# A decoder layer's SBUF pools laid out anew: where the moving operands of the matmuls begin

## Chip, cores and metric

The kernel runs on one core of a Trainium2 chip. The metric is the device time of one execution in microseconds; the median of three runs of the kernel before is 1162.74 us (1161.46 to 1162.74).

## What is computed

The reference is one decoder layer on x [512 tokens, 1024], float32:

```python
x = x + 0.5 * swiglu(rmsnorm(x, norm_ffn1), ffn1_gate, ffn1_up, ffn1_down)      # d_ff = 2816
h = rmsnorm(x, norm_mix)
qa, ka, va, qb, kb, vb, g_a, g_b = split(h @ w_in)
y_a = dilated_window_attention(qa, ka, va)     # 12 heads of 64, three groups merged
y_b = moba_attention(qb, kb, vb)               # 8 heads of 64, causal at this length
merged = sigmoid(g_a) * (y_a @ w_up_a) + sigmoid(g_b) * (y_b @ w_up_b)
x = x + merged @ w_out
x = x + 0.5 * swiglu(rmsnorm(x, norm_ffn2), ffn2_gate, ffn2_up, ffn2_down)
return rmsnorm(x, norm_final)
```

## The kernel before

The residual stream lies transposed in SBUF: eight tiles x0 to x7 of 128 partitions by 512 tokens. A projection takes a 128x128 piece of the weights as the stationary operand and a tile of 128x512 (all tokens) as the moving one. Every float32 operand is split into two float32r tiles, hi and lo, and `mac` (L196 to L201) issues three matmuls for each pair: hi*hi (L199), weight hi * moving lo (L200), weight lo * moving hi (L201). So each matmul of a projection has its own weight load, and the moving tiles are xh/xl (the normed stream), ah/al (the activations of the feed-forward halves, 22 pairs, pool `ff0` or `ff2`), yh/yl (the attention's outputs, 6 pairs) and mh/ml (the merged mixers, 8 pairs; both in pool `mrg`).

The stages in order: gate and up of the first half (`ffn(0)`, moving xh/xl), its down projection (moving ah/al), the projections of queries, keys and values and the two attentions with more projections blended in between (`blend`, tables FIRST and BESIDE), gates and merge (`ups`, moving yh/yl), the output projection (moving mh/ml), then the second half in the same way, whose last tile (`last_tile`) is done in two halves of 256 tokens, and the last norm. In `values` (L488 on) the roles are turned: the stream is stationary and 256 columns of the weights (whi/wlo) move; consecutive pieces of 256 columns are 1024 bytes apart.

In the attention the moving operands are ks (keys, from pool `op`) in the score products (L538, L550, L596), the identity in the transposes of the probability rows (L621), and pth/ptl (transposed rows) in the sums of values (L640); the stationary ones are qs, the rows prow and the values v. `bias` (L511) makes a tile of slopes times distances on POOL, read by VectorE when it adds it to the scores; one head of the dilated attention takes two tiles of 256 columns (tags `biasb`, `biasd`), each pair of MoBA heads two tiles of 512 (tag `bias`); every tag has two buffers.

Pools are laid one behind the other in the order in which they are opened, each tag taking its size rounded up to 32 bytes. `cpool`, `xpool`, `wpool` and `tpool` stay open for the whole program; `ff0`, then `op`, `mp` and `mp2`, then `mrg` in place of `mp` and `mp2`, and then `ff2` lie behind `tpool`. The 16-byte columns `rcol` and the 32-byte `nv` are tags of `tpool` (L217, L335), 128 bytes in all, behind its 2048-byte tiles. TensorE's order is written by hand (`manual_schedule`, PE only); the other engines' order is the scheduler's.

Where the tiles begin, in bytes of a partition, in the built program before and in the changed one:

| tiles | first byte before | mod 2048, mod 256 | first byte after | mod 2048, mod 256 |
|---|---|---|---|---|
| x, xh, xl (first: x0) | 18176 | 1792, 0 | 18432 | 0, 0 |
| whi, wlo | 79616 | 1792, 0 | 79872 | 0, 0 |
| tags ssq, fu, fg, rrow of tpool | 96000 | 1792, 0 | 96256 | 0, 0 |
| ah, al | 108416 | 1920, 128 | 108544 | 0, 0 |
| qs, ks (op) | 120704 | 1920, 128 | 120832 | 0, 0 |
| yh, yl (mrg) | 157568 | 1920, 128 | 157696 | 0, 0 |
| mh, ml (mrg) | 182144 | 1920, 128 | 182272 | 0, 0 |
| v | 162720 | 928 or 1952, 160 | 163072 | 256 or 1280, 0 |
| prow | 170912 | 928 or 1952, 160 | 171264 | 256 or 1280, 0 |
| pth, ptl | 212640 | 1696, 160 | 212992 | 0, 0 |
| ident, ones, ones_r | 16640 | 256, 768 or 1280, 0 | 16640 | 256, 768 or 1280, 0 |

Of the kernel before, what the change touches and what calls it, by code (L numbers as in the profile page):

```python
"""One core: a macaron SwiGLU pair around a gated merge of dilated window attention and MoBA.

The residual stream is kept transposed, [d_model on partitions, tokens], so that every projection
takes the weights as the stationary operand and the tokens as the moving one. A float32 operand is
split exactly into two float32r parts (hi + lo, 12 significant bits each); a product is the sum of
hi*hi, hi*lo and lo*hi, added up in float32 in PSUM. Query-key and probability-value products are
small and carry all four parts, hi and lo stacked on the partitions.

The RMSNorm's row factor is applied to the outputs of the projections that follow it, its gain to
their inputs. With MOBA_TOPK >= the number of blocks every past block is selected, so MoBA is causal  # L10
attention here. The three groups of the dilated attention are one softmax over their joint keys.
"""
# [11 lines left out]
F32 = mybir.dt.float32  # L24
# [4 lines left out]
P = 128  # L29
# [8 lines left out]
NT = S // P  # L38
EPS = 1e-6
BIG = 1e30  # L40
# Heads by pairs, as they are projected: those of the dilated attention, then MoBA's.
# [3 lines left out]
def by_class(ap):  # L45
    """[P, tokens] as [P, class t % 4, t // 4]."""
    return ap.rearrange("p (i r) -> p r i", r=NT)
# [10 lines left out]
# The projections of the mixers: those before the attention, and those beside each part of it  # L58
# (scores and weighted sums of each head of the dilated attention, then of each pair of MoBA's).
# [14 lines left out]
def blend(main, side, lead=0):  # L74
    """Run a generator beside others: `lead` steps of the others, then the rest spread over those of `main`.

    Each comes with its number of steps."""
    (main, total), left = main, sum(n for _, n in side) - lead
    steps = (None for g, _ in side for _ in g)
    done = 0  # L80
    for _ in range(lead):
        next(steps, None)
    for at in range(1, total + 1):
        while done * total < left * at:
            next(steps, None)
            done += 1
        next(main, None)
    for _ in main:
        pass
    for _ in steps:  # L90
        pass
# [3 lines left out]
def decoder_layer(ctx: ExitStack, tc: tile.TileContext, xT, gains, gus, gu1, dn1, wqk, wv, wg, wup, wout, gu2, dn2, base, out):  # L95
# [20 lines left out]
    def warm_up(n):  # L116
        """Keep the tensor engine's clock up while it waits."""
        ps = bank("all")
        for _ in range(n):
            nc.tensor.matmul(ps[:, :P], ones, ones, start=True, stop=True)  # L120

# [65 lines left out]
    def weights(*key):  # L187
        """The next tile of the stream, split, with the ones after it on their way."""
        t = state["at"]
        assert stream[t][0] == key, (t, stream[t][0], key)  # L190
        state["at"] += 1
        split(t + 1)
        fetch(t + 3)
        return splits.pop(t)

    def mac(ps, w, x, first, last):  # L196
        """ps += w.T @ x for split operands."""
        (wh, wl), (xh, xl) = w, x
        nc.tensor.matmul(ps, wh, xh, start=first, stop=False)  # L199
        nc.tensor.matmul(ps, wh, xl, start=False, stop=False)  # L200
        nc.tensor.matmul(ps, wl, xh, start=False, stop=last)  # L201
# [8 lines left out]
    def normed(i, k):  # L210
        """Tile k of the stream times the gain, split; and its part of the sum of squares."""
        xh = xpool.tile([P, S], F32R, name=f"xh{i}_{k}", tag=f"xh{k}")
        xl = xpool.tile([P, S], F32R, name=f"xl{i}_{k}", tag=f"xl{k}")
        g = g_sb[:, i * KT + k:i * KT + k + 1]
        nc.scalar.mul(xh, X[k], g)
        nc.vector.scalar_tensor_tensor(xl, X[k], g, f32(xh), ALU.mult, ALU.subtract)
        XN[k] = xh, xl  # L217
# [10 lines left out]
    def newton(y, z, a, out):  # L228
        """out = 1/sqrt(a): a step from the reciprocal of the table's square root."""
# [6 lines left out]
    def factors(i, ps):  # L236
        """1/rms of each token, as rows on all partitions."""
# [14 lines left out]
    def columns(row, dilated):  # L252
        """The same as columns [token of the tile, tile], tiles of 128 tokens or of a class of tokens."""
        col = tpool.tile([P, NT], F32, name="rcol", tag=f"rcol{dilated}", bufs=1)
# [6 lines left out]
    def tokens(x, t, dilated):  # L261
        """Tile t of the tokens of x [P, tokens]."""
        return by_class(x)[:, t] if dilated else x[:, t * P:(t + 1) * P]

# [1 line left out]
    def first_tiles():  # L266
        """Gate and up of the first two tiles, side by side over k as x comes in."""
# [60 lines left out]
    def last_tile(A):  # L328
        """The last tile of the stream in two halves of the tokens, each followed by its part of the output."""
# [6 lines left out]
        v = [tpool.tile([P, 4, 2], F32, name=f"nv{h}", tag=f"nv{h}", bufs=1) for h in range(2)]  # L336
# [92 lines left out]
    with ExitStack() as mix:  # L429
# [5 lines left out]
        consts = mp.tile([P, base.shape[-1]], F32, name="consts", tag="consts")  # L435
        nc.scalar.dma_start(consts, base)
# [8 lines left out]
        def project(t, j, which="acc"):  # L445
            """Queries (j = 0) or keys (j = 1) of a pair of heads, transposed."""
# [6 lines left out]
        def stacked(t, j, ps):  # L453
            v = tpool.tile([P, S], F32, name="qkv", tag="ssq", bufs=1)
            # The scores are kept with the sign turned, as their minimum is then the softmax's bias.
# [8 lines left out]
            # For each head: q as [hi; lo], k as [hi; hi] and [lo; lo].  # L464
# [21 lines left out]
        def values(c):  # L486
            """Values of four heads, tokens on partitions, [hi | lo] per head."""
            # Two tiles of tokens share a bank: its first product clears it for both.  # L488
# [21 lines left out]
        def bias(tag, n, *parts):  # L510
            """Slopes times distances, in [P, n]."""  # L511
            b = mp2.tile([P, n], F32, name="bias", tag=tag)
# [4 lines left out]
        def row_of(row, ps, b, low, den):  # L517
            """exp(score - max) of a row of scores, with its turned maximum and its sum."""
# [3 lines left out]
        def dsa_scores(h, rows):  # L522
            """Rows of the joint softmax of head h of each of the three groups.

            The dilated groups go by the classes t % 4 of the tokens, in which all their keys lie."""
            bb = bias("biasb", 256, (BAND, sl_a[h], 0))
            bd = bias("biasd", 256, (DILATED[:, :P], sl_a[4 + h], 0), (DILATED[:, P:], sl_a[8 + h], P))
            # [low or sum, own or other, by tiles or by classes, tile]
# [5 lines left out]
            for r in range(NT):  # L534
# [5 lines left out]
                # The two parts of the keys side by side: one long product instead of two short ones.  # L540
# [13 lines left out]
            # Each order of the tokens gets the other's minima and sums: a permutation, exact as it adds zeros.  # L554
# [32 lines left out]
        def moba_scores(heads, rows):  # L587
            """Rows of the softmax of each head over all keys up to its own."""
            bs = [bias("bias", 512, (CAUSAL, sl_b[h], 0)) for h in heads]
# [15 lines left out]
        def weighted(steps, ytile, half, classes=False):  # L605
            """The rows' sums of values, transposed, into half a tile of y.

            A step is up to four blocks of the rows to transpose, and the products that they go into:
            (tile of values, columns of y, first column, number of columns). Where the columns of y go by
            classes of tokens, products of 128-token tiles have theirs put into that order."""  # L610
# [47 lines left out]
        def dsa(h):  # L658
            """Scores and weighted sums of a head of the dilated attention, each with its number of steps."""
# [9 lines left out]
            # Tiles 0 and 2 of the keys cover the bank once; the others then add to all that they touch.  # L669
# [9 lines left out]
        def moba(h):  # L679
            """The same of a pair of heads of MoBA."""  # L680
# [31 lines left out]
        def part(what, n, *js):  # L712
            """Projections named in FIRST or BESIDE, with their number of steps."""
# [7 lines left out]
        # The first pair comes before the norm's factor is there.  # L721
# [73 lines left out]
def _tiles(w, heads=None):  # L795
    """[K, N] -> [N/128, 128, K]: for each tile of outputs, its K/128 stationary tiles side by side."""
# [4 lines left out]
def _moving(w, per):  # L801
    """[1024, n] -> [8/per, 128, per * n]."""
# [4 lines left out]
def _base():  # L807
    """Distances to a key, BIG where masked, and permutations of the tokens (see decoder_layer).

    Band of two tiles; classes t % 4 with dilations 4 and 16; all four tiles, ending with the query's."""  # L810
# [64 lines left out]
```

## Time and profile before

| what | value |
|---|---|
| median of the runs | 1162.74 us |
| span of the profiled execution | 1162.7 us |
| PE (matmul) busy | 1150.9 us, 5418 instructions |
| weight loads (PEld) busy | 966.8 us |
| VectorE busy | 597.9 us (51%) |
| ScalarE busy | 413.5 us (36%) |
| HBM traffic | 103.44 MB read, 91 GB/s over the span |

The profile gives no time of its own for this execution beside its span, which is that of the median run to 0.1 us. Matmuls are pipelined: a row's duration reaches into the next row, so the pace of the engine is read from the distance of the starts, and differences of durations between rows are used beside it.

### The profile page before, as it was taken

How to read it: one execution, taken by the hardware profiler on the slowest of the kernel's cores; microseconds unless marked ns; L12 is line 12 of the kernel's file. 1: busy time of each engine (PE TensorE's matmuls, PEld its weight loads, DVE VectorE, ACT ScalarE, POOL GpSimd, SP SyncE). 2: the span in 40 equal slices, each digit the busy share in tenths (PEclk: the TensorE clock that was granted, in tenths of full speed). 3: DMA queues.
4: the chain of work that ended last, by engine and by line, in shares of the span. 5: the costliest groups of instructions: out<-in, count | busy, mean ns of one | idle time of the engine just before them, and what ended most of it. 6: DMA issues, size and time to landing. Idle time of an engine off the chain costs nothing.

```text
span 1162.7 us, 13714 instructions
## 1 busy us (share of the span) xinstructions
PE 1150.9 (99%) x5418; PEld 966.8 (83%) x5418; DVE 597.9 (51%) x975; ACT 413.5 (36%) x641; POOL 19.6 (2%) x35
## 2 busy tenths in 40 slices
PE   8999999999999999999999999999999999999997
PEld 7888888888888899888998888888888888888886
DVE  5745444433333633777677667754744444433223
ACT  5433233222222323544454445433422323322222
POOL 0000000000000100000000000000000000000001
PEclk9999999999999999999999999999999999999999
DMA  5232232233233461446364222332233233233321
GB/s 200 93 107 91 95 105 91 94 97 100 87 99 122 140 173 55 128 127 164 111 162 127 74 64 82 110 99 99 91 96 104 91 96 103 91 100 84 98 82 73
DMA packets 37599, 122.14 MB, mean 105 GB/s; under 512 B 4752, under 2 KB 4768, under 8 KB 37536
## 3 DMA queue, kind: packets, MB, share of 16 engines
q1 hardware_dynamic: 37072, 120.08, 34.3%
q10 hardware_dynamic: 432, 1.18, 0.3%
q8 instruction: 42, 0.69, 0.2%
q14 instruction: 21, 0.17, 0.0%
q0 software_dynamic: 32, 0.02, 0.0%
HBM read 103.44 MB, written 2.10 MB: 91 GB/s over the span
## 4 chain that ended last, share of the span: by engine, by line
PE 98%; DVE 0%; DMA 0%; ACT 0%; issue 0%; DVEq 0%; POOLq 0%
PE ps_all L199 20%; PE ps_all L201 20%; PE ps_all L200 20%; PE ps_acc L199 9%; PE ps_acc L201 9%; PE ps_acc L200 9%; PE ps_all L276 2%; PE ps_out L640 2%; PE ps_att L621 1%; PE ps_att L199 1%; PE ps_att L200 1%; PE ps_att L201 1%; PE ps_att L596 1%; DMA g_sb<-in_gains_dram 0%; PE ps_att L538 0%; PE ps_att L550 0%
## 5 line engine op out<-in xcount | busy, mean ns | idle before, releaser
L182 ACT CAST whi<-raw 128x1024 fp32r<-128x1024 f32 (+2 forms) x201 | 202.8, 1010 | 562.4 <-PE ps_all L200 259.9
L183 DVE TENSOR_TENSOR wlo<-raw,whi 128x1024 fp32r<-128x1024 f32 (+2 forms) x202 | 236.2, 1170 | 174.1 <-ACT whi L182 174.0
L200 PE MATMUL ps_all<-xl,whi 128*128 128x512 f32 x672 | 261.4, 389 | 0.0
L199 PE MATMUL ps_all<-xh,whi 128*128 128x512 f32 x672 | 261.4, 389 | 0.0
L201 PE MATMUL ps_all<-xh,wlo 128*128 128x512 f32 x672 | 261.4, 389 | 0.0
L200 PEld LDWEIGHTS ps_all<-xl,whi 128*128 128x128 f32 x672 | 126.1, 188 | 26.3
L201 PEld LDWEIGHTS ps_all<-xh,wlo 128*128 128x128 f32 x672 | 126.1, 188 | 26.3
L199 PEld LDWEIGHTS ps_all<-xh,whi 128*128 128x128 f32 x672 | 126.1, 188 | 26.0
L199 PE MATMUL ps_all<-ah,whi 128*128 128x512 f32 (+1 forms) x374 | 143.1, 383 | 0.0
L200 PE MATMUL ps_all<-al,whi 128*128 128x512 f32 (+1 forms) x374 | 142.7, 382 | 0.0
L201 PE MATMUL ps_all<-ah,wlo 128*128 128x512 f32 (+1 forms) x374 | 142.7, 382 | 0.0
L199 PE MATMUL ps_acc<-xh,whi 128*128 128x512 f32 x272 | 110.2, 405 | 0.0
L201 PE MATMUL ps_acc<-xh,wlo 128*128 128x512 f32 x272 | 106.9, 393 | 0.0
L200 PE MATMUL ps_acc<-xl,whi 128*128 128x512 f32 x272 | 106.4, 391 | 0.0
L290 DVE TENSOR_TENSOR fu<-ps_all,rrow 128x512 f32<-128x512 f32 x44 | 30.4, 691 | 124.1 <-PE ps_all L201 124.1
L200 PEld LDWEIGHTS ps_all<-al,whi 128*128 128x128 f32 x374 | 70.2, 188 | 15.2
L201 PEld LDWEIGHTS ps_all<-ah,wlo 128*128 128x128 f32 x374 | 70.2, 188 | 15.1
L199 PEld LDWEIGHTS ps_all<-ah,whi 128*128 128x128 f32 x374 | 70.2, 188 | 15.0
L288 DVE TENSOR_TENSOR fg<-ps_all,rrow 128x512 f32<-128x512 f32 x44 | 30.4, 691 | 79.8 <-PE ps_all L201 79.7
L201 PEld LDWEIGHTS ps_acc<-xh,wlo 128*128 128x128 f32 x272 | 51.0, 188 | 11.3
L200 PEld LDWEIGHTS ps_acc<-xl,whi 128*128 128x128 f32 x272 | 51.3, 189 | 7.4
L199 PEld LDWEIGHTS ps_acc<-xh,whi 128*128 128x128 f32 x272 | 51.3, 188 | 7.4
(158 smaller groups left out, 1321.3 us busy)
## 6 DMA issues: line engine op xcount, KB each, us to landing
raw<-in_gu_dram SPq DMA_DIRECT2D x84, 512.0 KB, 3.4
raw<-in_dn_dram SPq DMA_DIRECT2D x32, 512.0 KB, 3.5
raw<-in_wqk_dram SPq DMA_DIRECT2D x20, 512.0 KB, 3.5
ks<-qkhl SPq DMA_DIRECT2D x40, 256.0 KB, 4.9
raw<-in_wg_dram SPq DMA_DIRECT2D x16, 512.0 KB, 3.5
raw<-in_dn_dram SPq DMA_DIRECT2D x16, 384.0 KB, 3.1
raw<-in_wv_dram SPq DMA_DIRECT2D x10, 512.0 KB, 4.0
qs<-qkhl SPq DMA_DIRECT2D x40, 128.0 KB, 2.6
```

Source lines behind the costliest of these rows:

```text
L182: nc.scalar.copy(hi[:, s], raw[:, s])
L183: nc.vector.tensor_tensor(lo[:, s], raw[:, s], f32(hi[:, s]), ALU.subtract)
L199: nc.tensor.matmul(ps, wh, xh, start=first, stop=False)
L200: nc.tensor.matmul(ps, wh, xl, start=False, stop=False)
L201: nc.tensor.matmul(ps, wl, xh, start=False, stop=last)
L276: nc.tensor.matmul(ps[j], w[:, at:at + P], x, start=k == 0 and n == 0, stop=k == KT - 1 and n == 2)
L288: nc.vector.tensor_tensor(g, ps[0], R, ALU.mult)
L290: nc.vector.tensor_tensor(u, ps[1], R, ALU.mult)
L596: nc.tensor.matmul(ps[:, :n], Q[NA + h][:, i * P:(i + 1) * P], K[NA + h][:, part, :n], start=part == 0, stop=part == 1)
L621: nc.tensor.transpose(pt[:, n * P:(n + 1) * P], block, ident)
L640: nc.tensor.matmul(to(po), V[v[0], v[1] // 4][:, v[1] % 4 * P:(v[1] % 4 + 1) * P], x[:, first:first + n], start=done == 1, stop=done == 2 ...
```

## The change

The small columns move from `tpool` into `cpool`, with 128 bytes more (`round`) that no code reads, so that `xpool` and all behind it begin at 18432 in place of 18176; `tpool` then ends with a 2048-byte tile. The tile of constants in `mp` grows from 1288 to 1344 columns, of which the same 1288 are loaded. `bias` has one tag of 512 columns in place of three. Comments and docstrings are gone from the file, so the lines' numbers shift by 5. What each instruction computes stays.

```diff
+    cols_of = {}
+    for name, shape in (("rcol0", [P, NT]), ("rcol1", [P, NT]), ("nv0", [P, 4, 2]), ("nv1", [P, 4, 2]), ("round", [P, 32])):
+        cols_of[name] = cpool.tile(shape, F32, name=name)
...
-        col = tpool.tile([P, NT], F32, name="rcol", tag=f"rcol{dilated}", bufs=1)
+        col = cols_of[f"rcol{int(dilated)}"]
...
-        v = [tpool.tile([P, 4, 2], F32, name=f"nv{h}", tag=f"nv{h}", bufs=1) for h in range(2)]
+        v = [cols_of[f"nv{h}"] for h in range(2)]
...
-        consts = mp.tile([P, base.shape[-1]], F32, name="consts", tag="consts")
-        nc.scalar.dma_start(consts, base)
+        consts = mp.tile([P, 1344], F32, name="consts", tag="consts")
+        nc.scalar.dma_start(consts[:, :base.shape[-1]], base)
...
-        def bias(tag, n, *parts):
-            b = mp2.tile([P, n], F32, name="bias", tag=tag)
+        def bias(*parts):
+            b = mp2.tile([P, 512], F32, name="bias", tag="bias")
...
-            bb = bias("biasb", 256, (BAND, sl_a[h], 0))
-            bd = bias("biasd", 256, (DILATED[:, :P], sl_a[4 + h], 0), (DILATED[:, P:], sl_a[8 + h], P))
+            both = bias((BAND, sl_a[h], 0), (DILATED[:, :P], sl_a[4 + h], 256), (DILATED[:, P:], sl_a[8 + h], 256 + P))
+            bb, bd = both[:, :256], both[:, 256:]
...
-            bs = [bias("bias", 512, (CAUSAL, sl_b[h], 0)) for h in heads]
+            bs = [bias((CAUSAL, sl_b[h], 0)) for h in heads]
```

On PE, VectorE, ScalarE and SyncE the instructions stand in the same order in both programs. On POOL the tiles of bias change places. Before, POOL's part for the two attentions (128x256 and 128x128 are one dilated head's, 128x512 one MoBA head's):

```order
L514 TENSOR_SCALAR bias<-consts 128x256
L514 TENSOR_SCALAR bias<-consts 128x128 x2
L514 TENSOR_SCALAR bias<-consts 128x256
L514 TENSOR_SCALAR bias<-consts 128x128 x2
L514 TENSOR_SCALAR bias<-consts 128x512 x2
L514 TENSOR_SCALAR bias<-consts 128x128 x2
L514 TENSOR_SCALAR bias<-consts 128x256
L514 TENSOR_SCALAR bias<-consts 128x128 x2
L514 TENSOR_SCALAR bias<-consts 128x256
L514 TENSOR_SCALAR bias<-consts 128x512 x6
```

and in the changed program:

```order
L519 TENSOR_SCALAR bias<-consts 128x256
L519 TENSOR_SCALAR bias<-consts 128x128 x2
L519 TENSOR_SCALAR bias<-consts 128x256
L519 TENSOR_SCALAR bias<-consts 128x128 x2
L519 TENSOR_SCALAR bias<-consts 128x256
L519 TENSOR_SCALAR bias<-consts 128x128 x2
L519 TENSOR_SCALAR bias<-consts 128x256
L519 TENSOR_SCALAR bias<-consts 128x128 x2
L519 TENSOR_SCALAR bias<-consts 128x512 x8
```

The first two MoBA tiles, which stood ahead of the third dilated head's, now come after all four heads', and each takes the buffer of a dilated head.

## Rows read from the trace of the kernel before

**Rows 1.** The page: busy time by engine, TensorE's granted clock, the chain that ended last.

```profile
PE 1150.9 (99%) x5418; PEld 966.8 (83%) x5418; DVE 597.9 (51%) x975; ACT 413.5 (36%) x641; POOL 19.6 (2%) x35
...
PEclk9999999999999999999999999999999999999999
...
PE 98%; DVE 0%; DMA 0%; ACT 0%; issue 0%; DVEq 0%; POOLq 0%
```

**Rows 2.** Waits of PE: waiter, waited for, us in total, times, longest.

```profile
PE ps_all L276 <- ACT xh L215: 2.3, 1, 2.3
...
PE ps_att L538 <- issue: 0.3, 1, 0.3
```

**Rows 3.** Windows (us; busy and count by engine, clock, DMA share, GB/s): down, attention.

```profile
280.00:360.00 80.00, 80.00 (x344) 64.36 (x344) 28.98 (x33) 22.67 (x28) 0.00 (x0) 1.00 0.32 97
...
460.00:711.00 251.00, 250.73 (x1392) 216.49 (x1391) 176.44 (x425) 120.78 (x248) 7.52 (x9) 1.00 0.42 116
```

**Rows 4.** Timeline of PE (start us, us) in gate and up.

```profile
99.67 0.39 PE L200 MATMUL ps_all<-xl,whi 128*128 128x512 f32 x1
...
105.79 0.39 PE L200 MATMUL ps_all<-xl,whi 128*128 128x512 f32 x1
```

**Rows 5.** Timeline of PE in the down projection.

```profile
249.72 0.40 PE L199 MATMUL ps_all<-ah,whi 128*128 128x512 f32 x1
...
255.78 0.40 PE L201 MATMUL ps_all<-ah,wlo 128*128 128x512 f32 x1
```

**Rows 6.** Groups by line and shape, whole span: count, busy us, mean ns.

```profile
L200 PE MATMUL ps_all<-xl,whi 128*128 128x512 f32 x672 | 261.4, 389 | 0.0
...
L201 PE MATMUL ps_all<-ah,wlo 128*128 128x512 f32 x330 | 130.3, 395 | 0.0
...
L200 PE MATMUL ps_acc<-xl,whi 128*128 128x512 f32 x272 | 106.4, 391 | 0.0
...
L199 PE MATMUL ps_acc<-mh,whi 128*128 128x512 f32 x64 | 25.3, 395 | 0.0
...
L201 PE MATMUL ps_att<-yh,wlo 128*128 128x512 f32 x48 | 19.0, 395 | 0.0
...
L200 PE MATMUL ps_att<-xl,whi 128*128 128x512 f32 x16 | 6.2, 389 | 0.0
```

**Rows 7.** Timeline of PE in the values, moving weights of 256 columns.

```profile
455.61 0.28 PE L199 MATMUL ps_acc<-whi,xh 128*128 128x256 f32 x1
...
457.04 0.28 PE L199 MATMUL ps_acc<-whi,xh 128*128 128x256 f32 x1
...
458.48 0.28 PE L199 MATMUL ps_acc<-whi,xh 128*128 128x256 f32 x1
```

**Rows 8.** Timeline of PE in the last tile, moving halves of 256 tokens.

```profile
1133.55 0.28 PE L199 MATMUL ps_all<-ah,whi 128*128 128x256 f32 x1
...
1135.93 0.28 PE L201 MATMUL ps_all<-ah,wlo 128*128 128x256 f32 x1
```

**Rows 9.** Timeline of PE in the first tiles, four matmuls to a row.

```profile
13.51 1.09 PE L276 MATMUL ps_all<-xh,wlo 128*128 128x512 f32 x4
14.43 1.08 PE L276 MATMUL ps_all<-xl,whi 128*128 128x512 f32 x4
15.35 0.61 PE L276 MATMUL ps_all<-xh,whi 128*128 128x512 f32 x2
```

**Rows 10.** Groups by line and shape, 460 to 711 us (both attentions).

```profile
L201 PE MATMUL ps_acc<-xh,wlo 128*128 128x512 f32 x240 | 94.5, 394 | 0.0
L200 PE MATMUL ps_acc<-xl,whi 128*128 128x512 f32 x240 | 94.0, 391 | 0.0
```

**Rows 11.** Timeline of VectorE, 540 to 600 us: two readers of bias.

```profile
557.55 0.43 DVE L519 CUSTOM_DVE_ANT_0 prow<-ps_att,bias 128x256 f32<-128x256 f32 x1 [0.88 <-PE ps_att L550]
...
581.08 0.69 DVE L519 CUSTOM_DVE_ANT_0 prow<-ps_att,bias 128x512 f32<-128x512 f32 x1
```

**Rows 12.** Timeline of POOL: one MoBA tile of bias.

```profile
593.26 1.55 POOL L514 TENSOR_SCALAR bias<-consts 128x512 f32<-128x512 f32 x1 [1.42 <-DVE low L519]
```

## The prediction

> **What bounds the kernel.** I read the page first: PE is busy for 1150.9 of 1162.7 us, the chain that ended last runs 98% on PE, and the granted clock stands at its upper level in every slice [rows 1]. The waits of PE come next: five in all, from 2.3 us down to 0.3, under 6 us together, and none of them in a projection [rows 2]. So nothing is to be had from waits: the time is the number of matmuls times the distance at which one follows the other, and a change that moves no instruction on PE can act only through that distance. It is read from the starts in the timeline, stage by stage.
>
> In gate and up the 28 rows from 99.67 to 105.79 us make 27 steps in 6.12 us: **226.7 ns** for a matmul of 512 columns [rows 4]. In the down projection the 27 rows from 249.72 to 255.78 make 26 steps in 6.06 us: **233.1 ns** [rows 5]. Same shape, same weight tiles, same clock of 1.00 [rows 1, 3]; only the moving tile differs, xh/xl against ah/al. By the table of addresses xh/xl begin on a multiple of 256 (1792 mod 2048), ah/al 128 bytes past one (1920). The groups by shape say the same of every family. The moving tiles 128 bytes past a multiple have 395 ns: ah/al (three groups of 330, alike), mh/ml (three of 64) and yh/yl (three of 48). The stream has 389, in gate and up and also where it goes into the banks of the attention (ps_att, 16 a group) [rows 6]. mh/ml into ps_acc and xh/xl into ps_att tell that neither the bank group nor the stage makes the difference: the moving tile does, by its offset or by its place in SBUF.
>
> Other engines have room where the pace would rise: in 80 us of the down projection VectorE is busy for 28.98, ScalarE for 22.67, and the DMA engines for 0.32 of the time [rows 3]. A pace 3% quicker is covered.
>
> **The change, part by part.**
>
> 1. *Moving tiles that leave the offset of 128.* 3 x 330 + 3 x 64 + 3 x 48 = 1326 matmuls of 512 columns now begin on multiples of 2048, and so of 256. If the offset is the cause, each goes from 233.1 to 226.7 ns: 1326 x 6.4 = **-8.5 us**. All of them lie on the path that sets the end, since PE waits nowhere there. The difference of durations, 395 - 389 = 6 [rows 6], gives -8.0; with starts known to 0.01 us, the distance may be 7, which gives -9.3. These are the ends.
>
> 2. *Moving tiles that go from 1792 to 0 mod 2048* (the stream and whi/wlo). They were multiples of 256 before. What a start on a multiple of 2048 does for 512 columns no row shows, but the values do for 256. There one k takes 12 matmuls and the pieces of the weights begin at 1792 and at 768 in turn. Those at 1792 run across a multiple of 2048, those at 768 do not. The 12 from 455.61 take 1.43 us (these at 1792), the 12 from 457.04 take 1.44 (at 768): 119 and 120 ns, no difference [rows 7]. I take 0; both ends are rivals below.
>
> 3. *The halves of the last tile.* ah/al in pieces of 256 tokens now begin at 0 and 1024. Before, with the offset of 128, 20 steps from 1133.55 took 2.38 us, 119 ns [rows 8]; the aligned weights of 256 columns took 120 [rows 7]. 132 x 1 ns = **+0.1 us**. So at 256 columns the offset costs nothing, which speaks a little against the first step: there the price is seen at 512 columns only.
>
> 4. *The attention.* Here the blended projections have an aligned moving tile already and yet take longer than in gate and up: L201 394 and L200 391 ns, 240 each, over 389 [rows 10], (5 + 2) x 240 = 1.7 us. Two causes are in the rows. One is that the stationary rows, queries and values beside them lie 160 or 128 bytes past a multiple of 256, and the change ends that. The other is a mere change of rhythm: in the first tiles, where all is on multiples of 256, eight matmuls after a slow stretch took (15.35 - 13.51) / 8 = 230 ns [rows 9] before the pace fell to 226.7. That stays, as short transposes still stand between. I take half: **-0.8 us**. The ends are -1.7 us and, if the new addresses bring the 480 to the 395 of the down rows, (1 + 4) x 240 = +1.2. The few score and value products with moving ks, pth and ptl (32 of 512 columns) add at most 0.2 either way.
>
> 5. *Bias.* In place of running ahead, the first MoBA tiles wait for a dilated head's buffer. The last dilated head's last read starts at 557.55 and takes 0.43 us; the first MoBA reader starts at 581.08 [rows 11]; a tile takes up to 1.55 us on POOL [rows 12]. Two tiles are done by some 562, with 19 us to spare: 0. If that cover were gone, the scores of a MoBA pair, and PE behind them, would wait the 3.1 us of two tiles, once. POOL has nothing else queued there.
>
> 6. *Columns in another pool, 56 columns more in constants, and the DMA as before:* no instruction is added; the small tiles are read by VectorE and ScalarE, which are off the path. 0.
>
> Sum: 1162.7 - 8.5 - 0.8 + 0.1 = **1153.5 us**. The span is the median to 0.1 us, so the sum stands against both.
>
> **The rivals.**
>
> *Place, not offset.* Every tile that goes slowly lies above byte 108416 and every one at 226.7 below it, so the trace cannot tell a byte offset of 128 from the far part of SBUF. Then the 1326 matmuls stay at 233.1 and nothing moves but the attention's 1.7 us at most: 1162.7, within 1.7. For it: the price is absent at 256 columns, where an offset should show too. Against it: step 4 has slower products whose moving tile lies below. The Trainium skill, "SBUF — State Buffer", section "Door 1: The DMA port swizzle", says that full bandwidth hangs on hitting the same 16-byte line twice, and each new line costs: 1792 and 1920 are both multiples of 16 and the runs are contiguous, so by that rule alone the two starts are equal and the time would stay; the trace has 226.7 against 233.1 between them, so the rule is not the whole of it.
>
> *A slower fit of moving and stationary reads.* The pace of the down rows may go with how the two operands' addresses stand to each other and to a 2048-byte line, and a start at 0 may be a worse one for the stream than 1792. Its price is that of the down rows: the stream's 3 x (672 + 272 + 16) and the 96 of the first tiles, 2976 matmuls, at 233.1 would cost 2976 x 6.4 = +19.0; with the 1326 unchanged that gives 1181.7. It decides from the first microseconds of gate and up, at any pace above about 230 ns. Against it: moving and weight tiles were both at 1792 in gate and up and are both at 0 now, so their distance is kept.
>
> *The line of 2048 matters too.* From 256 to 512 columns the aligned pace rises from 120 to 226.7 [rows 4, 7], 0.417 ns a column, so 512 columns alone are 213.3 and 13.3 ns are left over at both widths. If the left-over came of crossing a multiple of 2048, the 4302 products of 512 columns (2976 + 1326) would shed 13.3 each, 57 us more: about 1096. Against it: the pieces at 768 do not cross, and have it all the same [rows 7]. The Trainium skill, "TensorE: Matmul & The Clock Gate", section "Back-to-back issue gap", gives about 216 ns for 512 columns at the high clock; by that page the aligned products would have 11 ns each still to shed.
>
> **How the numbers follow.** Forecast 0.80, place 0.11, slower fit 0.05, line of 2048 0.04. The forecast's own ends are 1162.7 - 9.3 - 1.7 = 1151.7 and 1162.7 - 8.0 + 1.2 + 0.1 = 1156.0, with 0.2 for the small products and 0.2% (2.3 us), about what a measurement of this kernel tells from no change, partly on top: 1150.8 to 1158.0. That leaves out the rivals, 0.20. Faster: 0.80 + 0.04 = 0.84; within 0.2%: 0.11; slower: 0.05.
>
> **What would show it.** Right: in the down projection, the output projection and the merge the starts stand 226.7 ns apart and the groups of ah, mh and yh read 389 like the stream's; gate and up stays at 226.7; PE's waits stay as they are. Step 4 is right if L201 and L200 in the attention fall to about 391 and 390. Wrong: ah still at 395 (place), the stream above 389 (slower fit) or below 380 (line of 2048), or a wait of PE on VectorE's rows of the first MoBA pair (bias).

## The result, and the profile after

The changed kernel takes **1154.16 us** (median of 4 runs, 1153.87 to 1154.44) against 1162.74 before: ratio 0.9927, 95% interval 0.9915 to 0.9938, or 8.6 us less. Forecast were 1153.5 us and a range of 1150.8 to 1158.0. The profiled execution has a span of 1152.0 us (its time is 1154.17), 10.7 less than the span before. In every run with both on record the time is 1.7 to 2.2 us above the span, so the span before, 1162.7, belongs to an execution of about 1164.6 us (an estimate from these differences) and not to the median run of 1162.74: the 10.7 is some 2 us too much, and the medians decide.

The page of the changed kernel, parts 1 and 4, for [rows 1]:

```profile
PE 1140.5 (99%) x5418; PEld 966.1 (84%) x5418; DVE 598.3 (52%) x975; ACT 413.5 (36%) x641; POOL 19.9 (2%) x35
...
PE 98%; DVE 0%; DMA 0%; ACT 0%; issue 0%; DVEq 0%; POOLq 0%
```

PE is busy 10.4 us less with as many instructions; all other engines are where they were, and PE is still the chain. Its groups by line and shape (count, busy us, mean ns), for [rows 6]:

```profile
L205 PE MATMUL ps_all<-xl,whi 128*128 128x512 f32 x672 | 261.4, 389 | 0.0
...
L206 PE MATMUL ps_all<-ah,wlo 128*128 128x512 f32 x330 | 128.4, 389 | 0.0
...
L204 PE MATMUL ps_acc<-mh,whi 128*128 128x512 f32 x64 | 24.9, 389 | 0.0
...
L206 PE MATMUL ps_att<-yh,wlo 128*128 128x512 f32 x48 | 18.7, 389 | 0.0
```

The three families that stood at 395 read 389 now, and the stream reads 389 as before. The timeline of PE at the first product of the down projection, the first behind it, the first of the output projection, the first behind it, the first of the second down projection, and the first of the last tile's halves with the 21st of them:

```profile
248.44 0.39 PE L204 MATMUL ps_all<-ah,whi 128*128 128x512 f32 x1
...
368.12 0.39 PE L204 MATMUL ps_att<-xh,whi 128*128 128x512 f32 x1
...
734.63 0.39 PE L204 MATMUL ps_acc<-mh,whi 128*128 128x512 f32 x1
...
778.15 0.39 PE L204 MATMUL ps_all<-xh,whi 128*128 128x512 f32 x1
...
1017.96 0.39 PE L204 MATMUL ps_all<-ah,whi 128*128 128x512 f32 x1
...
1122.68 0.28 PE L204 MATMUL ps_all<-ah,whi 128*128 128x256 f32 x1
...
1125.07 0.28 PE L206 MATMUL ps_all<-ah,wlo 128*128 128x256 f32 x1
```

528 products in 119.68 us, 192 in 43.52, 462 in 104.72: 226.7 ns each. The same starts before, with 249.72 [rows 5] and 1133.55 [rows 8] as the first and the last:

```profile
372.92 0.39 PE L199 MATMUL ps_att<-xh,whi 128*128 128x512 f32 x1
...
741.13 0.40 PE L199 MATMUL ps_acc<-mh,whi 128*128 128x512 f32 x1
...
785.93 0.39 PE L199 MATMUL ps_all<-xh,whi 128*128 128x512 f32 x1
...
1025.76 0.40 PE L199 MATMUL ps_all<-ah,whi 128*128 128x512 f32 x1
```

They give 123.20, 44.80 and 107.79 us, 233.3 ns. Taken so from stage to stage, the span went down by 3.5 (first down projection), 0.9 (gates and merge), 1.3 (output projection), 3.1 (second down projection), 0.8 (projections and attentions) and 1.3 us (the first microseconds, see the end). Gate and up of the second half are unchanged to 0.03 us. The five stages make 9.6 us, 1.0 more than the medians; the first microseconds alone differ by more than that between executions of like kernels (see the end), so this rest is not resolved.

PE waits as before, five times, the first and the last of them:

```profile
PE ps_all L281 <- ACT xh L220: 2.0, 1, 2.0
...
PE ps_att L543 <- issue: 0.3, 1, 0.3
```

### The profile page after: what moved, and what is told of

Read it like the earlier page. It is cut to its first block, busy times and chain, and to the rows that moved or that the text cites. A ratio compares the mean times of both kernels' runs of the same rounds, so it can differ in the third digit from the quotient of the medians.

```text
span 1152.0 us, 13716 instructions
## 1 busy us (share of the span) xinstructions
PE 1140.5 (99%) x5418; PEld 966.1 (84%) x5418; DVE 598.3 (52%) x975; ACT 413.5 (36%) x641; POOL 19.9 (2%) x35
## 4 chain that ended last, share of the span: by engine, by line
PE 98%; DVE 0%; DMA 0%; ACT 0%; issue 0%; DVEq 0%; POOLq 0%
PE ps_all L204 20%; PE ps_all L205 20%; PE ps_all L206 20%; PE ps_acc L204 9%; PE ps_acc L206 9%; PE ps_acc L205 9%; PE ps_all L281 2%; PE ps_out L645 2%; PE ps_att L626 1%; PE ps_att L204 1%; PE ps_att L205 1%; PE ps_att L206 1%; PE ps_att L601 1%; DMA g_sb<-in_gains_dram 0%; PE ps_att L543 0%; PE ps_att L555 0%
## 5 line engine op out<-in xcount | busy, mean ns | idle before, releaser
L205 PE MATMUL ps_all<-xl,whi 128*128 128x512 f32 x672 | 261.4, 389 | 0.0
L206 PE MATMUL ps_all<-xh,wlo 128*128 128x512 f32 x672 | 261.4, 389 | 0.0
L206 PEld LDWEIGHTS ps_all<-xh,wlo 128*128 128x128 f32 x672 | 126.1, 188 | 26.3
L205 PEld LDWEIGHTS ps_all<-xl,whi 128*128 128x128 f32 x672 | 126.1, 188 | 26.0
L206 PE MATMUL ps_all<-ah,wlo 128*128 128x512 f32 (+1 forms) x374 | 140.8, 377 | 0.0
L205 PE MATMUL ps_all<-al,whi 128*128 128x512 f32 (+1 forms) x374 | 140.8, 376 | 0.0
L206 PE MATMUL ps_acc<-xh,wlo 128*128 128x512 f32 x272 | 106.4, 391 | 0.0
L205 PE MATMUL ps_acc<-xl,whi 128*128 128x512 f32 x272 | 106.3, 391 | 0.0
L206 PEld LDWEIGHTS ps_all<-ah,wlo 128*128 128x128 f32 x374 | 70.4, 188 | 13.0
L205 PEld LDWEIGHTS ps_all<-al,whi 128*128 128x128 f32 x374 | 70.4, 188 | 12.9
L206 PEld LDWEIGHTS ps_acc<-xh,wlo 128*128 128x128 f32 x272 | 51.1, 188 | 11.4
L205 PEld LDWEIGHTS ps_acc<-xl,whi 128*128 128x128 f32 x272 | 51.4, 189 | 7.2
```

## Experiments

The prediction took it that a start on a multiple of 256 bytes is quick and one 128 past it slow. Two theories give the same time for the change: the moving tile's **own offset** (mod 256, or mod 2048) and its **distance** from the stationary tile (mod 256). A third, its **place** in SBUF, would give it only if the change had ended the slowness of the far part in some other way. The runs shift one family at a time by unused tiles.

### The activations alone

```diff
         with tc.tile_pool(name=f"ff{i}", bufs=1) as apool:
+            apool.tile([P, 32], F32, name="shift", tag="shift")
```

> The changed kernel with an unused tile of 128 bytes at the start of the feed-forward halves' pool: ah/al begin at 128 mod 256, all else stays, and their place in SBUF moves by 128 bytes of some 108000. Offset theory: the 990 products of 512 columns of the two down projections go back from 226.7 to 233 ns apart, 395 ns in the groups in place of 389, +6.5 us over the changed kernel, about 1160.7. Place theory (the far part of SBUF was slow for another reason, which the change ended in some other way): 226.7 and 389 stay, 1154.2.

1160.28 us (1158.26 to 1161.88), 6.1 more than the changed kernel; groups of this kernel:

```profile
L204 PE MATMUL ps_all<-xh,whi 128*128 128x512 f32 x672 | 261.4, 389 | 0.0
...
L204 PE MATMUL ps_all<-ah,whi 128*128 128x512 f32 x330 | 130.3, 395 | 0.0
...
L204 PE MATMUL ps_acc<-mh,whi 128*128 128x512 f32 x64 | 24.9, 389 | 0.0
```

Place is out: 128 bytes bring the whole price back, and for the shifted family alone.

### The stream alone

The tile in `wpool` keeps whi and wlo on a multiple of 256.

```diff
+    wpool.tile([P, 32], F32, name="shift_w", tag="shift_w", bufs=1)
...
+    xpool.tile([P, 32], F32, name="shift_x", tag="shift_x")
     X = [xpool.tile([P, S], F32, name=f"x{k}", tag=f"x{k}") for k in range(KT)]
```

> 128 unused bytes ahead of the stream's tiles and 128 behind them: x, xh and xl begin at 128 mod 256, the weights and all behind them at multiples of 256 (256 mod 2048). Offset theory: the 2976 products of 512 columns with xh/xl moving, which lie in the near part of SBUF, go from 226.7 to 233 ns: +19 us, about 1173; ah, mh, yh stay at 226.7 though they begin at 256 and no longer at 0 mod 2048. Place theory: the stream stays at 226.7, the time at 1154. If the line of 2048 counts, ah, mh and yh rise too.

1168.26 us (1168.19 to 1168.5), 14.1 more. Its groups:

```profile
L205 PE MATMUL ps_all<-xh,whi 128*128 128x512 f32 x672 | 265.3, 395 | 0.0
...
L205 PE MATMUL ps_all<-ah,whi 128*128 128x512 f32 x330 | 128.4, 389 | 0.0
...
L205 PE MATMUL ps_acc<-mh,whi 128*128 128x512 f32 x64 | 24.9, 389 | 0.0
```

The stream, in the near part of SBUF, is now the slow one. ah and mh, at 256 mod 2048 here, stay quick: a multiple of 2048 is not needed. The price is under the 19 us expected mainly because the stage of the attentions lost 2.7 us (336.56 against 333.87), where its 864 products with the stream moving would lose 5.5 at 6.4 ns each. Why they lose less, no run shows.

### The weights alone, and everything

The second tile brings all that lies behind the weights back to multiples of 256.

```diff
+    wpool.tile([P, 32], F32, name="shift_w", tag="shift_w", bufs=1)
+    tpool.tile([P, 32], F32, name="shift_t", tag="shift_t", bufs=1)
```

> 128 unused bytes ahead of the weights' tiles and 128 behind them: whi/wlo begin at 128 mod 256, all moving tiles of 512 columns at multiples of 256. If the moving tile's own offset counts: 226.7 ns everywhere, 1154. If the distance between the moving and the stationary tile counts (they differ by 128 mod 256, as ah and whi did before): 233 ns in all 4302 products, +28 us, about 1182. The values, where the weights move with 256 columns at the offset of 128, should stay at 119 to 120 ns either way.

1175.37 us (1174.46 to 1176.27), 21.2 more, though every moving tile of 512 columns begins on a multiple of 256:

```profile
L206 PE MATMUL ps_all<-xh,whi 128*128 128x512 f32 x672 | 265.1, 395 | 0.0
...
L206 PE MATMUL ps_all<-ah,whi 128*128 128x512 f32 x330 | 130.2, 395 | 0.0
...
L206 PE MATMUL ps_acc<-mh,whi 128*128 128x512 f32 x64 | 25.3, 395 | 0.0
```

That is under the 28 us expected too: the attentions lost 2.3 us instead of 5.5, and gate and up went to 232.4 ns instead of 233. The values, where 256 columns of the shifted weights move against the unshifted stream, follow one another in 119 ns, against 120 in the changed kernel.

The other way round, one shift at the stream and none behind it takes everything from the stream on to 128 mod 256:

```diff
+    xpool.tile([P, 32], F32, name="shift_x", tag="shift_x")
```

> 128 unused bytes ahead of the stream's tiles and none behind: stream, weights, activations, merged tiles, keys, queries and values all begin at 128 mod 256, so moving and stationary tiles stand to each other as in the changed kernel. If the moving tile's own offset counts: 233 ns in all 4302 products, +28 us, about 1182. If the distance between the two counts: 226.7 ns everywhere, 1154.

1154.86 us (1154.39 to 1155.33), with no moving tile of 512 columns on a multiple of 256:

```profile
L204 PE MATMUL ps_all<-xh,whi 128*128 128x512 f32 x672 | 261.4, 389 | 0.0
...
L204 PE MATMUL ps_all<-ah,whi 128*128 128x512 f32 x330 | 128.4, 389 | 0.0
...
L204 PE MATMUL ps_acc<-mh,whi 128*128 128x512 f32 x64 | 24.9, 389 | 0.0
```

This pair settles it: with aligned moving tiles and shifted weights all families are slow, with everything shifted alike all are quick. Own offset is out, mod 256 and mod 2048, for the moving tile and for the weights; the **distance** between moving and stationary tile is what counts (taken mod 256 here; see below for the period).

### The least edit

```diff
+    cols_of = {}
+    for name, shape in (("rcol0", [P, NT]), ("rcol1", [P, NT]), ("nv0", [P, 4, 2]), ("nv1", [P, 4, 2])):
+        cols_of[name] = cpool.tile(shape, F32, name=name)
```

made to the kernel before, with its two uses, and nothing else: no tile `round`, the old constants and bias.

> The kernel before, with the small columns moved into the first pool and nothing else: the stream, weights, activations, merged tiles, keys and queries all begin at 128 mod 256 (1920 mod 2048), none at a multiple of 256, values and probability rows at 160 as before. Distance theory: all 4302 products of 512 columns at 226.7 ns, down projections, gates and merge and output projection as in the changed kernel; only what the attention gained, 0.8 us in the trace, may be missing: 1154.2 to 1155.5. If the multiples of 256 or 2048 count in themselves: 233 ns everywhere, about 1182.

1154.38 us (1152.26 to 1155.36), ratio to before 0.9921 (0.9904 to 0.9937): all of the gain. The 128 bytes of small columns at the end of `tpool` had set `ff0`, `op` and `mrg` 128 bytes off the weights. The round starts, the wider constants and the single bias tag add nothing that can be measured.

### Which distances

Three distances in one kernel each time, by shifts of `ff0`, `mrg` and `ff2`, in the first kernel by 32, 64 and 96 bytes:

```diff
+            apool.tile([P, 8 if i == 0 else 24], F32, name="shift", tag="shift")
...
+        mp.tile([P, 16], F32, name="shift_m", tag="shift_m")
```

> The changed kernel with unused columns at the start of three pools, weights at multiples of 256: ah/al of the first half at 32 bytes past one, yh/yl and mh/ml at 64, ah/al of the second half at 96. Distance theory (what counts is how far the moving tile lies from the stationary one, mod 256), in its plain form: each of these three distances is as slow as 128 was, 233 ns for 512 columns, 528, 336 and 462 products. Rival, that only half a line of 256 (128) is a bad distance: 226.7 for all three. A distance under 226.7 would be a better one than the change's.

> The same with 160 bytes (ah/al of the first half), 192 (yh/yl, mh/ml) and 224 (ah/al of the second half). Distance theory in its plain form: 233 ns for all three; if only 128 is bad: 226.7; if the price grows with the distance up to 256 or falls to both sides of 128, it shows between this run and the one before.

> The changed kernel with the moving tiles cut out of wider ones (2304 bytes) so that they begin 16 bytes past a multiple of 256 (ah/al of the first half), 8 bytes (yh, yl, mh, ml), 4 bytes (ah/al of the second half). If any distance off a multiple of 256 is slow, 233 ns in all three; if a distance inside some small line does no harm, 226.7 for those that are within it.

(In the last, `ah = tile[:, at:at + S]` with tiles of 576 columns in place of 512.) One run each: 1162.58, 1162.74 and 1163.97 us. The paces come from the starts of the stages' first products. For the first two distances of the first of these kernels they are these, 528 products between the first pair of rows, 192 between the second:

```profile
249.63 0.40 PE L204 MATMUL ps_all<-ah,whi 128*128 128x512 f32 x1
...
372.83 0.40 PE L204 MATMUL ps_att<-xh,whi 128*128 128x512 f32 x1
...
739.42 0.40 PE L204 MATMUL ps_acc<-mh,whi 128*128 128x512 f32 x1
...
783.37 0.40 PE L204 MATMUL ps_all<-xh,whi 128*128 128x512 f32 x1
```

| distance, mod 256 | products | us | ns each |
|---|---|---|---|
| 0 (changed kernel) | 528 | 119.68 | 226.7 |
| 4 | 462 | 109.33 | 236.6 |
| 8 | 192 | 44.80 | 233.3 |
| 16 | 528 | 122.31 | 231.6 |
| 32 | 528 | 123.20 | 233.3 |
| 64 | 192 | 43.95 | 228.9 |
| 96 | 462 | 107.82 | 233.4 |
| 128 (kernel before) | 528 | 123.20 | 233.3 |
| 160 | 528 | 123.70 | 234.3 |
| 192 | 192 | 44.80 | 233.3 |
| 224 | 462 | 107.80 | 233.3 |

Only 0 gives 226.7, and no distance tried is better; 64 stands out with a third of the price. That the distances repeat every 256 bytes is not shown: the pieces of 128 columns of the weights begin 512 bytes apart, all moving tiles counted under 0 are at 0 mod 512 from them, and no run had these tiles 256 mod 512 apart.

### The attention

> The changed kernel with the tile of constants at 1288 columns again: values, probability rows and pth/ptl begin at 32 mod 256, all else as in the changed kernel. Stationary rows and values then stand 32 bytes off the identity that moves against them and off the blended projections' weights. If step 4 of the prediction is right: up to 0.8 us more in the attention, 1154.2 to 1155; if the attention's gain came of keys and queries alone or is a change of rhythm: 1154.2.

```diff
-        consts = mp.tile([P, 1344], F32, name="consts", tag="consts")
+        consts = mp.tile([P, base.shape[-1]], F32, name="consts", tag="consts")
```

1154.47 us (1153.77 to 1155.10). The stage from the first product behind the down projection to the first of the merge:

```profile
368.10 0.39 PE L204 MATMUL ps_att<-xh,whi 128*128 128x512 f32 x1
...
701.67 0.39 PE L204 MATMUL ps_att<-yh,whi 128*128 128x512 f32 x1
```

333.57 us: values and probability rows at a distance of 32 from the weights cost nothing that shows. The end of the stage in the changed kernel (333.87 us from 368.12) and before (334.62 from 372.92):

```profile
701.99 0.39 PE L204 MATMUL ps_att<-yh,whi 128*128 128x512 f32 x1
```

```profile
707.54 0.40 PE L199 MATMUL ps_att<-yh,whi 128*128 128x512 f32 x1
```

Of the tiles of this stage keys and queries alone go back to 128:

```diff
+        op.tile([P, 32], F32, name="shift_o", tag="shift_o", bufs=1)
+        mp.tile([P, 32], F32, name="shift_m", tag="shift_m")
```

> The changed kernel with 128 unused bytes at the start of the pool of keys and queries, and 128 more ahead of the constants: keys and queries begin at 128 mod 256, values, probability rows and pth/ptl stay at multiples of 256; yh/yl and mh/ml, behind the same pool, go to 128 too. If the attention's gain comes of the distance between the blended projections and the keys and queries: the stage of the attentions goes from some 333.7 us (mean of the runs so far) back to 334.6; if not, it stays. Gates and merge and output projection go back to 33.6 and 44.8 us (+2.2).

One run, 1155.23 us. The same two starts:

```profile
366.38 0.39 PE L204 MATMUL ps_att<-xh,whi 128*128 128x512 f32 x1
...
700.98 0.40 PE L204 MATMUL ps_att<-yh,whi 128*128 128x512 f32 x1
```

334.60 us: as before the change. With keys and queries at distance 0 from the weights the stage took 333.4 to 334.0 us in nine kernels, with 128 it took 334.6 in two. Gates and merge and the output projection read 33.6 and 44.8 us here, as expected.

The starts show more closely where the price sits. 50 of the blended products, with xh and wlo at distance 0 from each other, have a score product behind them. From the start of such a product to the start of the next it is 232.8 ns on average before and 232.6 here, but 227.3 to 229.0 in the nine kernels. So a product's pace goes with the tiles of the product behind it too, not with its own pair alone; whether by that one's queries (the next weights) or its keys, these runs do not separate, as both were shifted together. By the starts these 50 steps make some 0.2 us of the 0.7; where the rest sits was not traced.

### Half a load (miss)

This kernel computes the first 64 rows of an output tile of the down projections and leaves out the other 64; ah/al of the second half begin 128 bytes further on.

```diff
+            if i == 2:
+                apool.tile([P, 32], F32, name="shift", tag="shift")
...
-                        mac(ps, cols(w, k - 8 * c), A[k], k == 0, k == FT - 1)
+                        mac(ps[:HD], [x[:, :HD] for x in cols(w, k - 8 * c)], A[k], k == 0, k == FT - 1)
-                nc.vector.scalar_tensor_tensor(X[m], ps, 0.5, X[m], ALU.mult, ALU.add)
+                nc.vector.scalar_tensor_tensor(X[m][:HD], ps[:HD], 0.5, X[m][:HD], ALU.mult, ALU.add)
```

> The changed kernel with 64 in place of 128 columns of weights loaded for each product of the down projections (the first 64 rows of each output tile alone are computed and added; the other 64 keep the old stream), ah/al at distance 0 in the first half and 128 in the second. Collision theory: the moving read and the load of the next weights get in each other's way, the 13.3 ns over 512 columns are the price of one load at distance 0, 20 ns at 128. Half a load should cost half: 220.0 ns in the first down projection (528 products, 116.2 us in place of 119.7) and about 223.3 in the second. Rival, a fixed price of a change of weights: 226.7 and 233.3 stay.

One run, 1157.85 us. At distance 0 the 528 products took 121.45 us, at 128 the 462 took 106.77:

```profile
248.54 0.40 PE L204 MATMUL ps_all<-ah,whi 128*64 128x512 f32 x1
...
369.99 0.39 PE L204 MATMUL ps_att<-xh,whi 128*128 128x512 f32 x1
...
1019.72 0.39 PE L204 MATMUL ps_all<-ah,whi 128*64 128x512 f32 x1
...
1126.49 0.28 PE L204 MATMUL ps_all<-ah,whi 128*128 128x256 f32 x1
```

230.0 and 231.1 ns: neither half the price (220.0 and 223.3) nor the same (226.7 and 233.3). Half a load at distance 0 is slower than a whole one. So the price is not in proportion to the columns loaded, nor a fixed one. That the pace goes with the distance, the pair of weights alone and everything shows; that the cause is two reads in each other's way is argued and not shown, and how the price comes about stays open.

## Why the prediction was right, and where it was not

- *What bounds the kernel:* right. PE's waits are the same, and the change acts through the distance of the starts alone. Two readings were off without harm: the longest of the five waits, 2.3 us, does stand in a projection, ahead of the first product of gate and up; and the span that the sum starts from is not that of the median run. As a change, the forecast is -9.2 us and the medians give -8.6.
- *Step 1,* -8.5 us by 1326 x 6.4: the four stages with ah, yh and mh gave 3.5 + 0.9 + 1.3 + 3.1 = 8.8. Size right, **cause wrong**. The step said "If the offset is the cause"; the runs show the distance from the weights instead. In the kernel before, the two could not be told apart: the weights lay at 1792, a multiple of 256, so an offset of 128 was a distance of 128 too. That the number came out is owed to this and not to the reason given.
- *Step 2,* 0 for 1792 to 0 mod 2048: right, gate and up stayed at 226.7 ns. The stream moves quickly at 1792, 0, 128 and 1920 mod 2048, so long as the weights begin at the same place mod 256.
- *Step 3,* +0.1 for the halves: right. 20 steps from 1122.68 to 1125.07 are 2.39 us, 119.5 ns, against 119 before [rows 8]. Over 60 steps it is 119.9 against 118.7. At 256 columns a distance of 128 costs nothing, and no run explains why.
- *Step 4,* -0.8 us: size right by taking half of a bound, and the cause was half right. It named "the stationary rows, queries and values" beside the projections; the queries and keys do it: they alone at 128 bring the whole 0.7 us back. Rows and values do nothing that shows at a distance of 32 from the weights (1288 columns of constants, and the least edit); at 160, as before, they were not tried by themselves. The expected fall, to 391 and 390, was seen in one of the two groups: in the attention, for [rows 10], L206 is down by 3 ns to 391, which is 0.7 us over 240 products, and L205 stays at 391:

```profile
L206 PE MATMUL ps_acc<-xh,wlo 128*128 128x512 f32 x240 | 94.0, 391 | 0.0
L205 PE MATMUL ps_acc<-xl,whi 128*128 128x512 f32 x240 | 93.9, 391 | 0.0
```

- *Step 5,* 0 for bias: right. POOL's second MoBA tile, and VectorE's first reading of one, for [rows 11, 12]:

```profile
553.23 0.62 POOL L519 TENSOR_SCALAR bias<-consts 128x512 f32<-128x512 f32 x1 [31.61 <-DVE st L524]
```

```profile
576.17 0.69 DVE L524 CUSTOM_DVE_ANT_0 prow<-ps_att,bias 128x512 f32<-128x512 f32 x1
```

  It waits 32 us for its buffer and is still 22 us early.
- *The rivals.* Place fell with the result, as the time did not stay, and with the first run. The slower fit described the true mechanism, "how the two operands' addresses stand to each other", and argued rightly that the distance is kept in gate and up; it was given 0.05 because it was tied to a worse start at 0. Its price is real: the weights alone, shifted, make the kernel 1.1% slower than before (ratio 1.0107, 1.0087 to 1.0127). The line of 2048 is out: gate and up keep 226.7 ns at 1792 and at 0, so the 13.3 ns left over at distance 0 are there still, and no run shows what they are. The 216 ns that the prediction took from the Trainium skill ("TensorE: Matmul & The Clock Gate", "Back-to-back issue gap") is that section's figure for a single matmul by itself; the products here stayed at 226.7. The Trainium skill's rule of 16-byte lines ("SBUF — State Buffer", "Door 1: The DMA port swizzle") does not tell quick from slow here: 16, 32 and 128 bytes, all multiples of 16, cost 5 to 7 ns.

## What to carry to other kernels

Where each matmul loads its own weights, read the distance of the starts: two paces for one shape at one granted clock can be a matter of layout. Look at where the moving and the stationary tile begin relative to each other before rounding anything (a multiple of 512 bytes apart was quick here, 256 was not tried); small tiles at the end of a pool are enough to set all later pools off. Here 128 bytes in another pool were worth 0.7%, and a distance of 0 was the best of eleven; at 256 columns it did not matter.

## What was not expected of the hardware

- The address of the weights changes the pace of the matmuls: 226.7 to 232.4 ns in gate and up (the last 957 products ahead of the first down projection, in 216.92 and 222.39 us) by moving whi/wlo alone by 128 bytes. The Trainium skill, "TensorE: Matmul & The Clock Gate", section "Step-by-step: what each phase is for", says "Loading the next tile's weights doesn't steal SBUF read bandwidth from the running matmul."; the runs differ from that in so far as the pace depends on where the weights lie, and they decide here; whether read bandwidth is the reason, they do not show.
- The first products after the start stand 427 ns apart for a while: in the changed kernel the four from 8.72 us (the last of them 399), and then 230 ns:

```profile
8.72 1.84 PE L281 MATMUL ps_all<-xh,wlo 128*128 128x512 f32 x4
10.40 1.09 PE L281 MATMUL ps_all<-xl,whi 128*128 128x512 f32 x4
11.32 1.09 PE L281 MATMUL ps_all<-xh,whi 128*128 128x512 f32 x4
```

  The view of windows gives a granted clock of 1.00 here, but this is no reading: the trace of the changed kernel has no record of the clock before 10.35 us. The trace with the weights alone shifted has one. There the eight products from 7.83 to 11.21 us, four to a row, take 422 ns each, and the granted clock is 0.50, the lower of the two levels (1.2 GHz):

```profile
7.83 1.88 PE L283 MATMUL ps_all<-xh,wlo 128*128 128x512 f32 x4
...
11.21 1.11 PE L283 MATMUL ps_all<-xh,whi 128*128 128x512 f32 x4
```

```profile
8.00:11.00 3.00, 3.00 (x9) 2.35 (x8) 3.00 (x6) 3.00 (x6) 0.00 (x0) 0.50 1.03 406
```

  PE had waited 2.1 us for xh before it and then run four products at the quick pace. With the activations alone shifted the window from 9 to 11 us reads 0.50 as well, at the same pace. So the slow start is the clock's lower level in these two; in the changed kernel and before it is the same pace without a record, and that the clock is its cause there is argued. The kernel before still had it in the four from 10.70. How long it lasts differs from one execution to the next: the 33rd matmul starts at 13.51 us before [rows 9], at 12.25 after, at 13.37 with everything shifted and at 10.51 with the keys shifted, in no order with the layout. The 1.3 us that the span lost there beside the stages is of this kind.
